# Gates, branch projections, q and k of an encoder block with tokens on partitions, turned back by TensorE

## The chip, the cores and the metric

One core of a Trainium2 chip runs the whole kernel. The metric is the device time in microseconds (us) of one execution, the median of several runs; lower is better. Engines are named as in the profile: PE is TensorE (PEld its weight loads), DVE is VectorE, ACT is ScalarE, POOL is GpSimd and SP is SyncE, which here issues the loads.

## What is computed

One layer of a bidirectional encoder block on 256 tokens of width 2048, all in float32:

```
xn = rms_norm(x, norm_pre_w)
z  = xn @ w_in                      # 2048 x 13312
u_lru, g_lru, q, k, v, g_attn, m_lru, m_attn = split(z)
u   = centred width-4 depthwise conv(u_lru)
h   = rg_lru(u, forward) + rg_lru(u, backward)
y_a = h * silu(g_lru)
q, k = partial_rope(q), partial_rope(k)     # first 32 of 128 dims of each head
y_b = windowed_gqa(q, k, v, sink) * silu(g_attn)    # 16 heads, 4 kv heads, |i-j| <= 128
merged = sigmoid(m_lru) * (y_a @ w_proj_a) + sigmoid(m_attn) * (y_b @ w_proj_b)
out = x + rms_norm(merged @ w_out, norm_post_w)
```

## The kernel before

Every weight is read once, 152 loads of 1 MB each in the order of `load_plan`. Each load is one step, each step two half-steps (hs, 304 in all). To keep float32 accuracy a weight tile is split into a high part wh (a cast on ACT, `parts_of`, L125) and a low part wl (a subtraction on DVE, L126), both in a format that PE multiplies in one pass. Activations are split likewise, and a product is three matmuls: high by high, high by low, low by high. The ring of split weights has five buffers, and the split for half-step hs + 4 is issued in half-step hs; raw loads have three buffers.

There are two ways to make a step:
- A **pair** (`add_pair`) makes 256 output features over two steps. The weights are stationary, the 256 tokens stream, and the result has features on partitions. In the wide form the activation's high and low parts lie side by side, so one 512-column matmul by wh makes two products at once in two halves of a PSUM bank, and a 256-column matmul by wl adds the third (L189, L190, L192); per slice of 128 input features these two alternate. `total` (L201, L202) then adds the two halves. In the narrow form, used for the first four ml pairs and the first gl pair, it is three 256-column matmuls.
- **Rows** (`add_rows`) makes 512 output features over four steps (a "quad" load). A 128-token slice of the activation is stationary, 512 columns of weights stream, and the result has tokens on partitions: 24 matmuls of 512 columns a step (`mm3`, L166 to L168). v and the output projection o are made so.

u's first 512 features have a form of their own (`u_quad`), during which the norm's sum of squares is formed. Until the norm is known, products use xs = x * norm_pre_w, and each pair result is multiplied afterwards by rbc, the reciprocal norm per token (`scaled`, L367); rows use rtok, the same per partition.

The order of all work is written by hand. `at(hs, fn)` and `soon(fn, d)` put work on other engines (and small matmuls on PE) into a half-step, ahead of that half-step's matmuls; each engine then runs its queue strictly in that order. The steps run: u quad; for eight groups ml (four of them), gl, ga, u pairs, with the LRU work of each group (`lru_pair`) spread over about 22 half-steps; k, v; then q pairs with pa and the rest of ml between, beside the 16 heads (`head`), one every four half-steps; then ma and pb, one after the other; then o. Names: ml and ma are the merge gates, gl and ga the silu gates, pa and pb the two branch projections, tm and sm the sigmoids of the merge gates, ms the merged result in two parts.

Of the kernel before, what the change touches and what calls it, by code (L numbers as in the profile page):

```python
# [14 lines left out]
F32 = mybir.dt.float32  # L15
F32R = mybir.dt.float32r
# [11 lines left out]
EPS = 1e-6  # L28
UNITS = 31
EARLY = 4  # L30
AHEAD = 4
DECAY = 12
SPIN = 10
G = 1
LRU0 = 12
HEAD0 = 5
# [15 lines left out]
def load_plan():  # L52

    plan = []

    def quad(m, c):
        plan.extend(("quad", m, c, i) for i in range(4))

    def pair(m, c, n):
        plan.extend(("blk", m, c + (n + i) * P, 0) for i in range(2))  # L60

    quad("w_in", U0)
    for i in range(8):
        if i < EARLY:
            pair("w_in", ML0, 2 * i)
        pair("w_in", GL0, 2 * i)
        pair("w_in", GA0, 2 * i)
        if i < 6:
            pair("w_in", U0, 2 * i + 4)
    pair("w_in", K0, 0)  # L70
    pair("w_in", K0, 2)
    quad("w_in", V0)
    fill = []
    for i in range(8):
        if i >= EARLY:
            fill.append(("w_in", ML0, 2 * i))
        fill.append(("w_proj_a", 0, 2 * i))
    for i in range(4):
        pair("w_in", Q0, 4 * i)
        pair("w_in", Q0, 4 * i + 2)  # L80
        for f in fill[2 * i:2 * i + 2]:
            pair(*f)
    for f in fill[8:]:
        pair(*f)
    for i in range(AHEAD):
        pair("w_in", MA0, 2 * i)
    for i in range(8):
        pair("w_proj_b", 0, 2 * i)
        if i + AHEAD < 8:
            pair("w_in", MA0, 2 * (i + AHEAD))  # L90
    for c in range(4):
        quad("w_out", c * 512)
    return plan


def body(ctx, tc, x, xT, wall, wlru, pvec, npost, ident_d, mask_d, rope_d, out):
# [47 lines left out]
    def soon(fn, d=1):  # L144
        at(now[0] + d, fn)
# [23 lines left out]

    def add_pair(name, act, done, spare=False, wide=True):  # L170


        got = {}

        def half(j, h, wh, wl):
            if j == 0 and h == 0:
                if wide:
                    got["ps"] = banks(name)
                else:
                    got["ps"] = bank(name) if spare else banks(name, (P, 2, S))  # L180
            ps = got["ps"][:, j]
            for k in range(8 * h, 8 * h + 8):
                sl = slice((k % 8) * P, (k % 8 + 1) * P)
                a = act[k // 2][:, k % 2]
                if not wide:
                    mm3(ps, wh[:, sl], wl[:, sl], a[:, 0], a[:, 1], k == 0, k == KT - 1)
                    continue
                if k > 0:
                    nc.tensor.matmul(ps[:, 1], wl[:, sl], a[:, 0], start=False, stop=False)  # L189
                nc.tensor.matmul(ps, wh[:, sl], a, start=k == 0, stop=k == KT - 1)  # L190
                if k == 0:
                    nc.tensor.matmul(ps[:, 1], wl[:, sl], a[:, 0], start=False, stop=False)  # L192
            if j == 1 and h == 1:
                soon(lambda: done(total(got["ps"]) if wide else got["ps"]))

        for j in range(2):
            steps.append(("blk", lambda h, wh, wl, j=j: half(j, h, wh, wl)))

    def total(ps):
        t = half_unit("total", "lo", F32, 1)  # L200
        nc.scalar.copy(t, ps[:, :, 1])  # L201
        nc.vector.tensor_tensor(t, ps[:, :, 0], t, ALU.add)  # L202
        return t

# [53 lines left out]
    mask = const.tile([P, 2, S], F32, name="mask")  # L258
    rope = const.tile([ROT, 2, S], F32, name="rope")
    rbc = const.tile([P, S], F32, name="rbc")  # L260
# [45 lines left out]
    def row_scale():  # L306
# [3 lines left out]
        nc.vector.reciprocal(rbc, rbc)  # L310

    for j in range(4):
        at(j // 2, lambda j=j: scale_x(2, j))
# [16 lines left out]

    at(40, token_scale)

    def load_tables():
        nc.sync.dma_start(ident, ident_d)
        nc.sync.dma_start(mask, mask_d)
        nc.sync.dma_start(rope, rope_d)
# [160 lines left out]
    def silu_evac(units_list, n):  # L497
        def done(ps):
            if n % 4 == 0:
                units_list.append(unit(f"sg{n}"))  # L500
            dst = units_list[n // 4][:, n % 4:n % 4 + 2]
            sg = half_unit(f"sig{n}", "p")
            scaled(dst, ps)
            nc.scalar.activation(sg, dst, AF.Sigmoid)
            nc.vector.tensor_tensor(dst, dst, sg, ALU.mult)
        return done

    tm, sm, ms = [], [], []

    def gate_evac(units_list, n):  # L510
        def done(ps):
            if n % 4 == 0:
                units_list.append(unit(f"mg{n}"))
            t = units_list[n // 4][:, n % 4:n % 4 + 2]
            scaled(t, ps)
            nc.scalar.activation(t, t, AF.Sigmoid)
        return done

    add_ml = lambda i, spare=False: add_pair(f"ml{i}", xs, gate_evac(tm, 2 * i), spare, i >= EARLY)
    b = LRU0  # L520
    for c in range(8):
        if c < EARLY:
            add_ml(c, c == 0)
        add_pair(f"gl{2 * c}", xs, silu_evac(sgl, 2 * c), c == 0, c > 0)
        add_pair(f"ga{2 * c}", xs, silu_evac(sga, 2 * c), c == 0 and EARLY == 0)
        if c < 6:
            n = 2 * c + 4
            add_pair(f"u{n}", xs, lambda ps, n=n: scaled(upad_tile(n)[:, :, 2:2 + S], ps))
        lru_pair(2 * c, b)
        b += 16 if c < EARLY else 12  # L530


    swap = [(i + 16) % 32 for i in range(32)]

    def add_heads(name, then):

        v = {}

        def evac(n):
            def done(ps):  # L540
                v[n] = half_unit(f"{name}f{n}", "uu")
                scaled(v[n], ps)
                for d in range(4):
                    soon(lambda d=d: rotate(n, d), d + 1)
            return done

        def rotate(n, d):
            t = v[n]
            r = t[0:ROT]
            if d == 0:  # L550
                v["s"] = small.tile([ROT, 2, S], F32, tag="upad", name=f"{name}s{n}", bufs=2)
                nc.vector.stream_shuffle(v["s"], r, swap)
                nc.vector.tensor_tensor(r, r, rope[:, 0].unsqueeze(1).to_broadcast([ROT, 2, S]), ALU.mult)
            elif d == 1:
                s = v["s"]
                nc.vector.tensor_tensor(s, s, rope[:, 1].unsqueeze(1).to_broadcast([ROT, 2, S]), ALU.mult)
                nc.vector.tensor_tensor(r, r, s, ALU.add)
            elif d == 2:
                if n == 0:
                    v["h"], v["l"] = unit(f"{name}h", F32R), unit(f"{name}l", F32R)  # L560
                parts_of(v["h"][:, n:n + 2], v["l"][:, n:n + 2], t)
            elif n == 2:
                then(v["h"], v["l"])
                v.clear()

        for n in (0, 2):
            add_pair(f"{name}{n}", xs, evac(n))

    kv = {}
    add_heads("k", lambda h, l: kv.update(kh=h, kl=l))  # L570

# [6 lines left out]

    add_rows("v_ps", xs, v_evac)

# [71 lines left out]

    def add_pa(i):
        def done(ps):
            t = tm[i // 2][:, i % 2 * 2:i % 2 * 2 + 2]
            nc.vector.tensor_tensor(t, ps, t, ALU.mult)

        add_pair(f"pa{i}", ya, done)

    def add_pb(i):  # L660
        def done(ps):
            ms.append(pair_unit(f"ms{i}"))
            t, g = (a[i // 2][:, i % 2 * 2:i % 2 * 2 + 2] for a in (tm, sm))
            nc.vector.tensor_tensor(g, ps, g, ALU.mult)
            nc.vector.tensor_tensor(g, t, g, ALU.add)
            parts_of(ms[i][:, :, 0], ms[i][:, :, 1], g)

        add_pair(f"pb{i}", yb, done)

    add_ma = lambda i: add_pair(f"ma{i}", xs, gate_evac(sm, 2 * i))  # L670
    fill = []
    for i in range(8):
        if i >= EARLY:
            fill.append((add_ml, i))
        fill.append((add_pa, i))
    for i in range(4):
        add_heads(f"q{i}", heads(i))
        for f, n in fill[2 * i:2 * i + 2]:
            f(n)
    for f, n in fill[8:]:  # L680
        f(n)
    for i in range(AHEAD):
        add_ma(i)
    for i in range(8):
        add_pb(i)
        if i + AHEAD < 8:
            add_ma(i + AHEAD)

# [81 lines left out]
def tables():  # L770
# [5 lines left out]
    c, s = np.cos(ang), np.sin(ang)  # L776
    rope = np.stack([np.concatenate([c, c]), np.concatenate([-s, s])], axis=1).astype(np.float32)
    return np.eye(P, dtype=np.float32), np.ascontiguousarray(mask), np.ascontiguousarray(rope)
# [41 lines left out]
```

## Time and profile before

| what | value |
|---|---|
| runs | 922.26 us median of 3 (922.04 to 922.36) |
| profiled execution, first to last instruction (span) | 920.5 us |
| PE busy, share of the span | 910.4 us, 99% |
| DVE busy | 679.9 us, 74% |
| ACT busy | 549.8 us, 60% |
| granted TensorE clock, mean | 0.997 |
| DMA | 172.28 MB, 187 GB/s |

The profile gives the profiled execution's span but no device time of its own; the runs lie 1.5 to 1.9 us above that span. PE's busy time counts overlapping matmuls as one stretch, so it says that PE always had a matmul under way, not how fast they follow each other; that is read from the starts of neighbouring matmuls.

### The profile page before, as it was taken

The page shows a single profiled execution, that of the slowest core. Times are in us where ns is not written, and L with a number is a line of the kernel's source. Part 1 is how long each engine was busy: PE and PEld are TensorE (multiplying, and loading weights), DVE is VectorE, ACT ScalarE, POOL GpSimd, SP SyncE. Part 2 cuts the span into 40 slices and gives each one's busy share as a digit, 9 for nine tenths or more (in the row PEclk, how much of TensorE's full clock was granted, in tenths as well). Part 3 has the DMA queues.
Part 4 walks back from the last instruction along what each step waited for, and adds up shares of the span by engine and source line. Part 5 has one row for each costly group of instructions (what it writes and reads, how often), then busy time and mean ns, then how long its engine had stood idle before and what let it go on. Part 6 is the DMA issues. An engine that isn't in the chain of part 4 may idle for free.

```text
span 920.5 us, 13471 instructions
## 1 busy us (share of the span) xinstructions
PE 910.4 (99%) x5398; PEld 804.2 (87%) x5398; DVE 679.9 (74%) x944; ACT 549.8 (60%) x775; POOL 1.4 (0%) x23
## 2 busy tenths in 40 slices
PE   8999999999999999999999999999999999999996
PEld 8999898988888888888888888888888888888885
DVE  6986868787879888898787868766675566665554
ACT  6758584949597967854544555666554444445451
POOL 0000000000000000000000000000000000000000
PEclk9999999999999999999999999999999999999998
DMA  9755455555464454456544445444555555559542
GB/s 327 256 206 198 141 199 182 207 176 213 142 247 169 165 207 147 162 204 229 183 162 160 143 177 175 146 164 156 183 183 183 185 188 184 192 189 341 185 138 91
DMA packets 27614, 172.28 MB, mean 187 GB/s; under 512 B 3072, under 2 KB 3840, under 8 KB 8480
## 3 DMA queue, kind: packets, MB, share of 16 engines
q1 hardware_dynamic: 26832, 170.27, 52.3%
q10 hardware_dynamic: 720, 1.16, 0.3%
q8 instruction: 42, 0.69, 0.3%
q14 instruction: 20, 0.16, 0.0%
HBM read 169.32 MB, written 2.10 MB: 186 GB/s over the span
## 4 chain that ended last, share of the span: by engine, by line
PE 98%; DMA 1%; DVE 0%; ACT 0%; SPq 0%; DVEq 0%; issue 0%
PE pb L190 7%; PE ga L190 7%; PE ma L190 6%; PE q L190 6%; PE pa L190 6%; PE gl L190 6%; PE u L190 5%; PE o L168 4%; PE o L167 4%; PE o L166 4%; PE ml L190 3%; PE pb L189 3%; PE ga L189 3%; PE ma L189 3%; PE pa L189 3%; PE q L189 3%
## 5 line engine op out<-in xcount | busy, mean ns | idle before, releaser
L126 DVE TENSOR_TENSOR wl<-raw,wh 128x1024 fp32r<-128x1024 f32 (+1 forms) x306 | 368.8, 1214 | 166.2 <-ACT wh L125 165.5
L125 ACT CAST wh<-raw 128x1024 fp32r<-128x1024 f32 (+1 forms) x305 | 312.5, 1042 | 118.8 <-PE o L168 31.1
L190 PE MATMUL ga<-xs,wh 128*128 128x512 f32 x256 | 90.5, 397 | 0.0
L190 PE MATMUL pb<-yb,wh 128*128 128x512 f32 x256 | 90.0, 398 | 0.0
L190 PE MATMUL ma<-xs,wh 128*128 128x512 f32 x256 | 89.9, 397 | 0.0
L190 PE MATMUL pa<-ya,wh 128*128 128x512 f32 x256 | 89.9, 396 | 0.0
L190 PE MATMUL q<-xs,wh 128*128 128x512 f32 x256 | 89.7, 396 | 0.0
L190 PE MATMUL gl<-xs,wh 128*128 128x512 f32 x224 | 78.9, 397 | 0.0
L189 PE MATMUL pb<-yb,wl 128*128 128x256 f32 x240 | 67.5, 281 | 0.0
L189 PE MATMUL ma<-xs,wl 128*128 128x256 f32 x240 | 67.4, 281 | 0.0
L189 PE MATMUL ga<-xs,wl 128*128 128x256 f32 x240 | 67.4, 281 | 0.0
L190 PE MATMUL u<-xs,wh 128*128 128x512 f32 x192 | 67.2, 395 | 0.0
L189 PE MATMUL q<-xs,wl 128*128 128x256 f32 x240 | 67.1, 279 | 0.0
L189 PE MATMUL pa<-ya,wl 128*128 128x256 f32 x240 | 67.1, 279 | 0.0
L189 PE MATMUL gl<-xs,wl 128*128 128x256 f32 x210 | 58.9, 280 | 0.0
L190 PEld LDWEIGHTS pb<-yb,wh 128*128 128x128 f32 x256 | 47.4, 188 | 10.5
L190 PEld LDWEIGHTS ga<-xs,wh 128*128 128x128 f32 x256 | 47.6, 188 | 10.2
L190 PEld LDWEIGHTS ma<-xs,wh 128*128 128x128 f32 x256 | 47.4, 188 | 10.2
L190 PEld LDWEIGHTS q<-xs,wh 128*128 128x128 f32 x256 | 47.4, 188 | 9.8
L190 PEld LDWEIGHTS pa<-ya,wh 128*128 128x128 f32 x256 | 47.4, 188 | 9.7
L189 PE MATMUL u<-xs,wl 128*128 128x256 f32 x180 | 50.3, 279 | 0.0
L166 PE MATMUL o<-wh,ms 128*128 128x512 f32 x128 | 49.8, 389 | 0.0
(267 smaller groups left out, 1958.0 us busy)
## 6 DMA issues: line engine op xcount, KB each, us to landing
raw<-wall_dram SPq DMA_DIRECT2D x149, 1024.0 KB, 4.8
lraw<-wlru_dram SPq DMA_DIRECT2D x8, 512.0 KB, 5.7
raw<-wall_dram SPq DMA_DIRECT2D x4, 512.0 KB, 7.6
xr<-x_dram SPq DMA_DIRECT2D x4, 512.0 KB, 10.2
raw<-wall_dram SPq DMA_DIRECT2D x4, 256.0 KB, 4.8
xT<-xT_dram SPq DMA_DIRECT2D x4, 256.0 KB, 7.0
np<-npost_dram SPq DMA_DIRECT2D x2, 512.0 KB, 8.0
out_dram<-yw SPq DMA_DIRECT2D x4, 256.0 KB, 2.3
```

The source lines that it names most:

```text
L125: cast(h, src)
L126: nc.vector.tensor_tensor(l, src, h.bitcast(F32), ALU.subtract)
L166: nc.tensor.matmul(ps, wh, xh, start=start, stop=False)
L167: nc.tensor.matmul(ps, wh, xl, start=False, stop=False)
L168: nc.tensor.matmul(ps, wl, xh, start=False, stop=stop)
L189: nc.tensor.matmul(ps[:, 1], wl[:, sl], a[:, 0], start=False, stop=False)
L190: nc.tensor.matmul(ps, wh[:, sl], a, start=k == 0, stop=k == KT - 1)
```

## The change

ml, ma, pa, pb, k and q become rows: 84 of the 152 steps go from the pair form to the rows form. gl, ga and the later u groups stay pairs. Where the features are needed on partitions afterwards (q and k for the scores, the merged result for o), PE turns the result with 128x128 transposes against the identity. x is normalised once: after the norm is known xT is scaled by norm_pre_w and rbc and split into xn, which later steps use instead of xs; the scaling of each pair result falls away. The rotary embedding works on token rows (`rotate`). In pairs the wide matmuls of a half-step come in a run of eight and the narrow ones in another, arranged so that runs of neighbouring half-steps join. The order of steps changes: u quad, ml's first quad, v, then the groups with the other ml quads between, k, then q and pa in turn, ma, pb, o.

```diff
-UNITS = 31
-EARLY = 4
-AHEAD = 4
+UNITS = 32
-LRU0 = 12
+LRU0 = 13
+BETWEEN = {1: 1, 3: 2, 5: 3}
+XN = 15
+PACE = (20,) + (16,) * 6 + (12,) * 2
...
     quad("w_in", U0)
+    quad("w_in", ML0)
+    quad("w_in", V0)
...
+    quad("w_in", K0)
+    for c in range(4):
+        quad("w_in", Q0 + c * 512)
+        quad("w_proj_a", c * 512)
+    for c in range(4):
+        quad("w_in", MA0 + c * 512)
+    for c in range(4):
+        quad("w_proj_b", c * 512)
...
-    def add_pair(name, act, done, spare=False, wide=True):
+    def add_pair(name, act, done):
...
+            def row(wide):
+                for k in range(8 * h, 8 * h + 8):
+                    sl = slice((k % 8) * P, (k % 8 + 1) * P)
+                    a = act[k // 2][:, k % 2]
+                    if wide:
+                        nc.tensor.matmul(ps, wh[:, sl], a, start=k == 0, stop=k == KT - 1)
+                    else:
+                        nc.tensor.matmul(ps[:, 1], wl[:, sl], a[:, 0], start=False, stop=False)
+
+            row(h == 0)
+            row(h == 1)
...
+    def weigh(i):
+        for j in range(4):
+            nc.scalar.activation(xt[i][:, j], xt[i][:, j], AF.Copy, scale=norm(4 * i + j))
+
+    def normal(i):
+        t = xt[i]
+        nc.vector.tensor_tensor(t, t, rbc.unsqueeze(1).to_broadcast([P, 4, S]), ALU.mult)
+
+    def xn_parts(i):
+        for j in range(2):
+            a = pair_unit(f"xn{2 * i + j}")
+            xn.append(a)
+            parts_of(a[:, :, 0], a[:, :, 1], xt[i][:, 2 * j:2 * j + 2])
+
+    for i in range(4):
+        at(7 + 2 * i, lambda i=i: weigh(i))
+        at(XN + 2 * i, lambda i=i: normal(i))
+        at(XN + 1 + 2 * i, lambda i=i: xn_parts(i))
...
-    at(40, token_scale)
+    at(ROWS + 3, token_scale)
+    at(6, lambda: nc.sync.dma_start(ident, ident_d))
...
+        def evac(t, ps):
+            if t == 0:
+                v["t"] = unit(f"{name}t", F32, (P, 2, 512))
+            nc.scalar.copy(v["t"][:, t], ps)
+            if t == 1:
+                soon(rotate)
+                soon(flip, 2)
+                for q in range(2):
+                    soon(lambda q=q: part(q), 3 + q)
...
+            nc.vector.tensor_tensor(m[:, :, :, 0:half], r[:, :, :, half:ROT], table(1, 0, half), ALU.mult)
+            nc.vector.tensor_tensor(m[:, :, :, half:ROT], r[:, :, :, 0:half], table(1, half, ROT), ALU.mult)
+            nc.vector.tensor_tensor(c, r[:, :, :, 0:ROT], table(0, 0, ROT), ALU.mult)
+            nc.vector.tensor_tensor(r[:, :, :, 0:ROT], c, m, ALU.add)
...
+        def flip():
+            for q in range(2):
+                v[q] = bank(f"{name}p{q}")
+                for j in range(2):
+                    n = 2 * q + j
+                    for t in range(2):
+                        nc.tensor.transpose(v[q][:, j, t * P:(t + 1) * P], v["t"][:, t, n * P:(n + 1) * P], ident)
...
+    def add_pb(c):
+        held = {}
+        def done(t, ps):
+            g = sm[c][:, t]
             nc.vector.tensor_tensor(g, ps, g, ALU.mult)
+            nc.vector.tensor_tensor(g, tm[c][:, t], g, ALU.add)
+            if t == 1:
+                soon(flip)
+                for q in range(2):
+                    soon(lambda q=q: part(q), 2 + q)
```

The order on PE in the pairs that stay. In the rows below a name is out<-streamed,stationary; gl is the PSUM tile, xs and xn the activation, wh and wl the weight parts. Before, the start of a gl pair:

```order
L190 MATMUL gl_1105<-xs_120,wh_0_975 128x512
L192 MATMUL gl_1105<-xs_120,wl_0_976 128x256
L189 MATMUL gl_1105<-xs_120,wl_0_976 128x256
L190 MATMUL gl_1105<-xs_120,wh_0_975 128x512
L189 MATMUL gl_1105<-xs_131,wl_0_976 128x256
L190 MATMUL gl_1105<-xs_131,wh_0_975 128x512
```

And now:

```order
L175 MATMUL gl_881<-xn_639,wh_0_761 128x512 x2
L175 MATMUL gl_881<-xn_642,wh_0_761 128x512 x2
L175 MATMUL gl_881<-xn_692,wh_0_761 128x512 x2
L175 MATMUL gl_881<-xn_695,wh_0_761 128x512 x2
L177 MATMUL gl_881<-xn_639,wl_0_762 128x256 x2
L177 MATMUL gl_881<-xn_642,wl_0_762 128x256 x2
```

Wide and narrow matmuls no longer alternate; sixteen of one kind follow sixteen of the other.

On DVE in the pb stage, where the merged result is formed and split (total is the sum of the two PSUM halves, mg a gate tile, ms the parts). Before:

```order
L202 TENSOR_TENSOR total<-pb_6904,total 128x512
L664 TENSOR_TENSOR mg_6601<-total,mg_6601 128x512
L665 TENSOR_TENSOR mg_6601<-mg_580,mg_6601 128x512
L126 TENSOR_TENSOR ms_6988<-mg_6601,ms_6988 128x2x256
L126 TENSOR_TENSOR wl_0_6994<-raw_6941,wh_0_6993 128x1024
```

And now, for one quad of pb; PE's two rows of four transposes each (`ms_ps<-ident,mg`, L694) stand a half-step behind the last L682 and ahead of that half-step's matmuls:

```order
L116 TENSOR_TENSOR wl_1_6601<-raw_6548,wh_1_6600 128x1024
L681 TENSOR_TENSOR mg_5936<-pb__6485,mg_5936 128x512
L682 TENSOR_TENSOR mg_5936<-mg_651,mg_5936 128x512
L681 TENSOR_TENSOR mg_5936<-pb__6485,mg_5936 128x512
L682 TENSOR_TENSOR mg_5936<-mg_651,mg_5936 128x512
L116 TENSOR_TENSOR wl_0_6623<-raw_6582,wh_0_6622 128x1024
L116 TENSOR_TENSOR wl_1_6650<-raw_6582,wh_1_6649 128x1024
L116 TENSOR_TENSOR ms_6667<-ms_ps_6639,ms_6667 128x2x256
```

PE now waits for DVE's four products before it turns the tile, and the split of ms moves behind the turn.

On DVE near half-steps 14 to 16, while the first LRU group starts (uu is the convolution, sp the decay constants, lwl the LRU weights' low part). Before:

```order
L424 SCALAR_TENSOR_TENSOR uu_575<-upad_535,pv,uu_575 128x256 x3
L126 TENSOR_TENSOR wl_1_619<-raw_501,wh_1_618 128x1024
L387 TENSOR_TENSOR sp_e<-sp_e,sp_den 128x32
L388 TENSOR_TENSOR sp_s_166<-sp_e 128x32
L126 TENSOR_TENSOR lwl_651<-lraw_442,lwh_650 128x1024
L126 TENSOR_TENSOR wl_0_655<-raw_571,wh_0_654 128x1024
L389 TENSOR_SCALAR sp_pl<-sp_s_166 128x32
```

And now:

```order
L432 SCALAR_TENSOR_TENSOR uu_569<-upad_513,pv,uu_569 128x256 x3
L116 TENSOR_TENSOR wl_0_599<-raw_537,wh_0_598 128x1024
L307 TENSOR_TENSOR xT_96<-xT_96,rbc 128x1024
L397 TENSOR_SCALAR sp_pl<-sp_s_166 128x32
L389 SCALAR_TENSOR_TENSOR sp_pl<-sp_pl,sp_s_166 128x32
L116 TENSOR_TENSOR lwl_618<-lraw_469,lwh_617 128x1024
L116 TENSOR_TENSOR wl_1_622<-raw_537,wh_1_621 128x1024
L116 TENSOR_TENSOR xn_639<-xT_96,xn_639 128x2x256
L116 TENSOR_TENSOR xn_642<-xT_96,xn_642 128x2x256
```

The multiplication by rbc and two subtractions for xn now stand between the weight splits, and the same again three more times.

More of the change, by code (lines that the diff above doesn't have):

```diff
@@ L62, in load_plan @@
     quad("w_in", U0)
+    quad("w_in", ML0)
+    quad("w_in", V0)
     for i in range(8):
-        if i < EARLY:
-            pair("w_in", ML0, 2 * i)
         pair("w_in", GL0, 2 * i)
@@ L69, in load_plan @@
             pair("w_in", U0, 2 * i + 4)
[L70 to L90, printed above, removed]
+        if i in BETWEEN:
+            quad("w_in", ML0 + BETWEEN[i] * 512)
+    quad("w_in", K0)
[6 more added lines that the diff above has]
+        quad("w_proj_b", c * 512)
     for c in range(4):
@@ L176, in half, with total @@
             if j == 0 and h == 0:
[L177 to L180, printed above, removed]
+                got["ps"] = banks(name)
             ps = got["ps"][:, j]
[L182 to L192, printed above, removed]
+            def row(wide):
[8 more added lines that the diff above has]
+            row(h == 1)
             if j == 1 and h == 1:
-                soon(lambda: done(total(got["ps"]) if wide else got["ps"]))
+                soon(lambda: done(got["ps"]))
         for j in range(2):
             steps.append(("blk", lambda h, wh, wl, j=j: half(j, h, wh, wl)))
-    def total(ps):
+    def total(dst, ps):
         t = half_unit("total", "lo", F32, 1)
         nc.scalar.copy(t, ps[:, :, 1])
-        nc.vector.tensor_tensor(t, ps[:, :, 0], t, ALU.add)
-        return t
+        nc.vector.tensor_tensor(dst, ps[:, :, 0], t, ALU.add)
     def add_rows(name, act, done, spare=False, last=False):
@@ L258, in body @@
     mask = const.tile([P, 2, S], F32, name="mask")
-    rope = const.tile([ROT, 2, S], F32, name="rope")
+    rope = const.tile([P, 2, 2, ROT], F32, name="rope")
     rbc = const.tile([P, S], F32, name="rbc")
@@ L310, in row_scale @@
         nc.vector.reciprocal(rbc, rbc)
+    xn = []
+    def weigh(i):
[13 more added lines that the diff above has]
+        at(XN + 1 + 2 * i, lambda i=i: xn_parts(i))
     for j in range(4):
@@ L329, in token_scale @@
             nc.scalar.activation(dg, dg, AF.Copy, accum_out=rtok[:, t:t + 1])
-    at(40, token_scale)
+    at(ROWS + 3, token_scale)
+    at(6, lambda: nc.sync.dma_start(ident, ident_d))
     def load_tables():
-        nc.sync.dma_start(ident, ident_d)
         nc.sync.dma_start(mask, mask_d)
@@ L502, in done, with u_evac @@
             sg = half_unit(f"sig{n}", "p")
-            scaled(dst, ps)
+            total(dst, ps)
             nc.scalar.activation(sg, dst, AF.Sigmoid)
-            nc.vector.tensor_tensor(dst, dst, sg, ALU.mult)
+            soon(lambda: nc.vector.tensor_tensor(dst, dst, sg, ALU.mult))
         return done
+    def u_evac(n):
+        return lambda ps: total(upad_tile(n)[:, :, 2:2 + S], ps)
     tm, sm, ms = [], [], []
[L510 to L516, printed above, removed]
-        return done
@@ L519, in body @@
[L519 to L530, printed above, removed]
@@ L533, in body @@
[L533 to L567, printed above, removed]
@@ L569, in body, with gate_evac @@
+    def gate_evac(units_list, c, scale=1.0):
+        def done(t, ps):
+            if t == 0:
+                units_list.append(unit(f"mg{c}", F32, (P, 2, 512)))
+            nc.scalar.activation(units_list[c][:, t], ps, AF.Sigmoid, scale=rtok[:, t:t + 1] if scale is None else scale)
+        return done
+    add_rows("ml0_", xs, gate_evac(tm, 0, None), True)
     kv = {}
-    add_heads("k", lambda h, l: kv.update(kh=h, kl=l))
     def v_evac(t, ps):
@@ L577, in v_evac @@
         nc.vector.scalar_tensor_tensor(vl, ps, rtok[:, t:t + 1], vh.bitcast(F32), ALU.mult, ALU.subtract)
-    add_rows("v_ps", xs, v_evac)
+    add_rows("v_", xs, v_evac)
+    b = LRU0
+    for c in range(8):
+        add_pair(f"gl{2 * c}", xn, silu_evac(sgl, 2 * c))
+        add_pair(f"ga{2 * c}", xn, silu_evac(sga, 2 * c))
+        if c < 6:
+            add_pair(f"u{2 * c + 4}", xn, u_evac(2 * c + 4))
+        if c in BETWEEN:
+            add_rows(f"ml{BETWEEN[c]}_", xn, gate_evac(tm, BETWEEN[c]))
+        lru_pair(2 * c, b)
+        b += PACE[c]
@@ new lines, in add_heads, with rotate, part @@
+    def add_heads(name, then):
+        v = {}
+        def evac(t, ps):
+            if t == 0:
+                v["t"] = unit(f"{name}t", F32, (P, 2, 512))
[5 more added lines that the diff above has]
+                    soon(lambda q=q: part(q), 3 + q)
+        def rotate():
+            r = v["t"].rearrange("p t (h d) -> p t h d", h=4)
+            both = small.tile([P, 2, 2, 4, ROT], F32, tag="turn", name=f"{name}r", bufs=1)
+            c, m = both[:, 0], both[:, 1]
+            table = lambda i, a, b: rope[:, :, i, a:b].unsqueeze(2).to_broadcast([P, 2, 4, b - a])
+            half = ROT // 2
+            nc.vector.tensor_tensor(m[:, :, :, 0:half], r[:, :, :, half:ROT], table(1, 0, half), ALU.mult)
[9 more added lines that the diff above has]
+                        nc.tensor.transpose(v[q][:, j, t * P:(t + 1) * P], v["t"][:, t, n * P:(n + 1) * P], ident)
+        def part(q):
+            if q == 0:
+                v["h"], v["l"] = unit(f"{name}h", F32R), unit(f"{name}l", F32R)
+            parts_of(v["h"][:, 2 * q:2 * q + 2], v["l"][:, 2 * q:2 * q + 2], v[q])
+            if q == 1:
+                then(v["h"], v["l"])
+                v.clear()
+        add_rows(f"{name}_", xn, evac)
@@ L581, in head @@
+    add_heads("k", lambda h, l: kv.update(kh=h, kl=l))
     def head(hd, qh, ql, b):
@@ L650, in heads, with add_pa, done, flip @@
         return then
[L653 to L675, printed above, removed]
+    def add_pa(c):
+        def done(t, ps):
+            g = tm[c][:, t]
+            nc.vector.tensor_tensor(g, ps, g, ALU.mult)
+        add_rows(f"pa{c}_", ya, done)
+    def add_pb(c):
+        held = {}
+        def done(t, ps):
+            g = sm[c][:, t]
+            nc.vector.tensor_tensor(g, ps, g, ALU.mult)
+            nc.vector.tensor_tensor(g, tm[c][:, t], g, ALU.add)
[3 more added lines that the diff above has]
+                    soon(lambda q=q: part(q), 2 + q)
+        def flip():
+            for q in range(2):
+                held[q] = bank(f"ms_ps{c}{q}")
+                for j in range(2):
+                    n = 2 * q + j
+                    for t in range(2):
+                        nc.tensor.transpose(held[q][:, j, t * P:(t + 1) * P], sm[c][:, t, n * P:(n + 1) * P], ident)
+        def part(q):
+            a = pair_unit(f"ms{2 * c + q}")
+            ms.append(a)
+            parts_of(a[:, :, 0], a[:, :, 1], held.pop(q))
+        add_rows(f"pb{c}_", yb, done)
     for i in range(4):
         add_heads(f"q{i}", heads(i))
[L678 to L684, printed above, removed]
+        add_pa(i)
+    for i in range(4):
+        add_rows(f"ma{i}_", xn, gate_evac(sm, i))
+    for i in range(4):
         add_pb(i)
-        if i + AHEAD < 8:
-            add_ma(i + AHEAD)
     npt, xr, yw = [], [[], []], [[], []]
@@ L776, in tables @@
     c, s = np.cos(ang), np.sin(ang)
-    rope = np.stack([np.concatenate([c, c]), np.concatenate([-s, s])], axis=1).astype(np.float32)
+    rope = np.stack([np.concatenate([c, c]), np.concatenate([-s, s])]).astype(np.float32)
+    rope = rope.reshape(2, ROT, 2, P).transpose(3, 2, 0, 1)
     return np.eye(P, dtype=np.float32), np.ascontiguousarray(mask), np.ascontiguousarray(rope)
```

## The prediction

> **What bounds the kernel now.** I read the page's first block and chain, then PE's own waits, then the chain in order of time, because what matters is how long PE needs from one product to the next.
>
> ```profile
> PE 910.4 (99%) x5398; PEld 804.2 (87%) x5398; DVE 679.9 (74%) x944; ACT 549.8 (60%) x775; POOL 1.4 (0%) x23
> PE 98%; DMA 1%; DVE 0%; ACT 0%; SPq 0%; DVEq 0%; issue 0%
> PE u_ps L352 <- ACT wh L125: 1.5, 2, 0.9
> ACT wh L125 <- PE pb L190: 14.2, 8, 1.8
> 912.86 0.24 PE o L168
> ```
>
> PE is the chain: 98% of the span, and its longest wait (two times, 1.5 us in all) lies in the first steps. ACT waits for PE to hand back weight buffers, so the weight path runs ahead of PE. From PE's last product (913.10) to the end at 920.5 lie 7.4 us that the change doesn't touch. So the question is PE's time per step, plus any new wait. A step is one MB of weights. It has two forms: 16 slices of a 512-column and a 256-column matmul (pair), or 24 matmuls of 512 columns (rows); both stream 12,288 columns.
>
> ```profile
> 684.65 0.46 PE ma L190 x2
> ...
> 692.40 0.24 PE pb L190
> 692.64 0.12 PE pb L189
> 692.76 0.23 PE pb L190
> ...
> 707.24 0.46 PE ma L190 x2
> L166 PE MATMUL o<-wh,ms x128: 389/389/389, 825.9 to 912.2; 128*128 128x512 f32 x128
> ```
>
> The first and last rows are the same place of two pairs, four steps apart: 22.59 us, so a wide pair step takes 5.648 us, 353 ns a slice. The o row gives the other form: one of three matmuls, 127 intervals in 86.3 us, 679.5 ns for three, 226.5 ns each; a rows step takes 5.44 us. PE is "busy" in both, so busy time doesn't show the difference.
>
> ```profile
> 42.80 0.28 PE L166 MATMUL gl<-xs,wh 128*128 128x256 f32 x1
> ...
> 50.72 0.28 PE L166 MATMUL gl<-xs,wh 128*128 128x256 f32 x1
> 368.49 0.28 PE L166 MATMUL gate<-uh,lwh 128*128 128x256 f32 x1
> ...
> 369.79 0.28 PE L168 MATMUL gate<-uh,lwl 128*128 128x256 f32 x1
> 370.07 0.24 PE v_ps L166
> 372.14 0.23 PE v_ps L166
> ```
>
> Runs of narrow matmuls: 66 intervals in 7.92 us (120 ns) and 11 in 1.30 us (118 ns). A narrow pair step (48 of them; the first four ml pairs and gl0) takes 5.76 us. The two v_ps rows are nine matmuls apart: 230 ns each for wide ones just after narrow ones, before they settle at 226.5.
>
> **Part 1: ml, ma, pa, pb, k and q as rows (84 of 152 steps).** ma and pb: 32 steps, 5.648 - 5.44 = 0.208 each, 6.6 us. k: 4 steps, 0.8. The narrow ml pairs: 8 steps, 0.32 each, 2.6. q, pa and the last ml pairs lie among the heads:
>
> ```profile
> 451.63 0.60 PE L616 MATMUL pt<-ident,p 128*128 128x128 f32 x4
> 451.99 0.36 PE L166 MATMUL sc<-kh,q0h 128*128 128x256 f32 x1
> 452.79 0.28 PE L189 MATMUL q<-xs,wl 128*128 128x256 f32 x1
> 451.80 0.44 PE pt L616 x4
> ...
> 647.30 0.44 PE pt L616 x4
> 450.00:655.00 205.00, 205.00 (x1258) 182.01 (x1257) 156.81 (x298) 114.18 (x188) 0.00 (x0) 1.00 0.47 165
> ```
>
> Fifteen heads in 195.5 us are 13.03 us each; of that 1.16 is pt and sc (451.63 to 452.79) and six o matmuls take 0.71, which leaves 5.58 for a step. So 40 steps gain 0.14: 5.6. Part 1 gives 15.6 us.
>
> **Part 2: pairs that stay (gl, ga, u), with wide and narrow matmuls in runs.** 44 steps. No row shows such a run of 16 and 16; bounds come from the rows above: 16 x (226.5 + 118) = 5.51 us and 16 x (230 + 120) = 5.60. I take 228.5 and 119, 5.56: a run begins as v_ps does and then settles. 42 wide steps gain 0.088 and gl0's two 0.2: 4.1 us (2.5 to 6.2; nothing, if the mix isn't what costs).
>
> **Part 3: the turns on PE.** Nine flips (k, four q, four pb) of eight 128x128 transposes: 72, all on the path. pt is the same instruction. The chain gives 0.44 us for four, 110 ns; from the starts (451.63 to 451.99) it is 90. I take 110: 7.9 us (6.5 to 8.3). The Trainium skill (TensorE: Matmul & The Clock Gate, Part 4: PE-mode transpose) puts one at about 275 ns in a kernel and says the full clock doesn't engage for it. The trace agrees with the length alone: 0.60 us from the first start to the last end of four which start 0.36 apart with their follower, and in the window 450 to 655, with 15 heads' transposes, the granted clock is 1.00. By the page's figure the flips would be an estimated 19.8 us.
>
> **Part 4: what DVE, ACT and the queues get.**
>
> ```profile
> L126 DVE TENSOR_TENSOR wl<-raw,wh 128x1024 fp32r<-128x1024 f32 x302 | 366.0, 1221 | 164.9 <-ACT wh L125 164.2
> L125 ACT CAST wh<-raw 128x1024 fp32r<-128x1024 f32 x302 | 310.6, 1047 | 117.6 <-PE o L168 31.1 <-PE ma L190 18.5 <-PE pb L190 14.2
> L367 DVE TENSOR_TENSOR sg<-total,rbc 128x512 f32<-128x512 f32 x15 | 10.4, 693 | 0.5
> L491 DVE TENSOR_TENSOR gi<-gi,th 128x1024 f32<-128x1024 f32 x8 | 9.7, 1218 | 0.0
> L126 DVE TENSOR_TENSOR yb<-sg,yb 128x512 fp32r<-128x512 f32 x8 | 5.5, 684 | 0.0
> L280 ACT ACTIVATE xs<-xT,pv 128x256 fp32r<-128x256 f32 x16 | 7.4, 503 | 3.5 <-DMA xT<-xT_dram 1.8 <-DMA pv<-pvec_dram 1.5
> L424 DVE SCALAR_TENSOR_TENSOR uu<-upad,pv,uu 128x256 f32<-128x256 f32 x48 | 23.3, 485 | 2.6 <-DVE uu L424 0.5
> ACT L309 <- PE rps L308: 2.4, 1, 2.4
> 27.43 1.22 DVE L299 TENSOR_TENSOR sq<-sq,sq 128x1024 f32<-128x1024 f32 x1
> 28.56 1.22 DVE L126 TENSOR_TENSOR wl<-raw,wh 128x1024 fp32r<-128x1024 f32 x1
> 48.54 1.23 DVE L126 TENSOR_TENSOR wl<-raw,wh 128x1024 fp32r<-128x1024 f32 x1 [1.63 <-ACT wh L125]
> ```
>
> Added once: xn, on ACT 16 scalings (503 ns) and 8 casts (somewhat over half of L125's 1.05, about 0.6), 13 us; on DVE 4 multiplies (nearest 1218) and 8 subtractions (684), 10.4 us. Removed: the L367 scaling of 48 pairs, 33 us of DVE, and the totals of what becomes rows; nothing of that was on the path. The new work is bunched in half-steps 7 to 22, and in 13 to 24 it meets the first LRU pair. There I count on DVE 12 splits, 4 multiplies, 8 subtractions, the convolution (8 of about 0.47, 3.7), lwl, ul, v, gated and small ones: some 37 us of durations, less 0.09 of overlap for each of 45 (27.43 to 28.56 is 1.13 for 1.22), so 33. PE needs 12 x 2.72 and 24 gate matmuls, 35.4. ACT comes to about the same 33, its table loads counted. That is 93%, with ACT and DVE waiting for each other. What covers it is the lead: the split at 48.54 is for half-step 16 and ends at 49.8; half-step 12 began at 42.80, and four narrow ones of 2.88 later is 54.3, a lead of 4.5. Served in turn, the lead shrinks to about 1 us near half-steps 20 and 28. I charge 0.5 (0 to 6).
>
> The scaling stands ahead of L309's Sqrt on ACT, which idled 2.4 us there for PE; it fits. ident's load moves from half-step 20 to 6 on SP's queue, ahead of one raw load; 64 KB among 1 MB loads that come two steps early: nothing. rope keeps its place and bytes.
>
> Each flip makes PE wait for other engines, with a whole half-step queued behind. For k and q the order is copy (half-step +1), rope (+2), flip (+3): DVE has PE's whole half-step for four small products (about 1.5 us). For pb it is tight:
>
> ```profile
> 690.00:825.00 135.00, 135.00 (x767) 117.26 (x766) 83.51 (x87) 62.53 (x72) 0.00 (x0) 1.00 0.53 185
> 748.38 0.69 DVE L664 TENSOR_TENSOR mg<-total,mg 128x512 f32<-128x512 f32 x1
> 749.10 0.69 DVE L665 TENSOR_TENSOR mg<-mg,mg 128x512 f32<-128x512 f32 x1
> ```
>
> Four products (two dependent pairs at 0.72 and 0.69, about 2.8 us) against PE's 2.72. But token half 0 is complete six matmuls (1.36 us) earlier, so DVE can begin before the half-step ends. I charge 0.1 for each of four, 0.4. For the last pb, o needs it four half-steps later.
>
> **Sum.** 15.6 + 4.1 - 7.9 - 0.5 - 0.4 = 10.9 us. The profiled span of 920.5 becomes 909.6. The runs (median 922.26) lie 1.8 us above the span, for what is outside it: **911.4 us**. As a check, adding steps for the kernel before in the same way comes to about 1 us more than its span.
>
> **Rivals.**
> - The jam: DVE and ACT lose the lead at half-steps 13 to 32 and PE waits 3 to 6 us. For: 93% load in turns. Against: durations overlap, and pairs after it need less DVE than before. 914 to 917.
> - Grouping gains nothing: the extra of the mix comes from narrow matmuls however they stand. For: they take 118 to 120 in runs, no less than beside wide ones. Against: the wide ones take 226.5 in runs and about 234 in the mix (353 less 119). 915.5.
> - Slower: the flips expose the whole chain ahead of them, because DVE comes to it only when its split is done. Each wait is then up to 2.8 us, nine of them 25 us: 935. It decides from 1.2 us a flip. Against: DVE is busy 84 of 135 us in the pb stage.
> - The change doesn't do what it says: time goes by columns alone, rows gain nothing, and the flips are added: about 931. The rows of 353 and 226.5 ns speak against it. The Trainium skill's rule (same page, Back-to-back issue gap: N/2.4 + 2.5 ns) gives just this, an estimated 5.20 us against 5.18 a step; the trace doesn't agree.
> - Transposes one after another at their whole length of 272 ns (0.60 less 0.33): 19.6 us, 923. pt's starts speak against it; the page on transposes stands nearest to it.
>
> **Chances.** Forecast (908 to 913.5) 0.62, jam 0.15, no gain by grouping 0.1, lower by cheap turns and runs 0.05; slower flips 0.03, columns alone 0.02, long transposes 0.03. A measurement here tells 0.2%, 1.8 us, from no change. Faster 0.92, same 0.02, slower 0.06. Range: low, 1.8 more from Part 2, 1.4 from cheaper turns, no waits: 907; high, the jam at 6: 917. Outside are some 0.15.
>
> **What would show it.** Rows cadence of 227 ns in pa and pb; a pair step of gl at 5.5 to 5.6; eight transposes in about 0.9 us; no wait of PE before L694's and L583's transposes over 0.3 us; DVE nearly full from 45 to 85 us without a PE wait. I am wrong if PE waits for wl or wh there, or if the pair steps stay at 5.65.

## The result, and the profile after

| kernel | time, median (range) | ratio to before, 95% interval | span |
|---|---|---|---|
| before | 922.15 us (921.61 to 922.36) | 1 | 920.5 us |
| changed | 914.65 us (914.31 to 915.47) | 0.9921 [0.9906, 0.9935] | 912.5 us |

The change gains 7.5 us, and 8.0 us of the profiled span; forecast were 10.9 us, and 911.4 us with a range of 907 to 917. The measured time lies in that range, but above the 908 to 913.5 that was given a chance of 0.62. The first rows of the changed kernel's page: busy time by engine, then the chain by engine.

```profile
PE 903.0 (99%) x4638; PEld 772.1 (85%) x4638; DVE 610.6 (67%) x841; ACT 551.7 (60%) x775; POOL 1.4 (0%) x23
PE 98%; DMA 1%; DVE 0%; ACT 0%; issue 0%; SPq 0%; DVEq 0%
```

PE is still the chain; that DVE has 69 us less to do lies off it. PE's waits in the changed kernel (total us, times, longest):

```profile
PE spin L240 <- POOL eps L235: 1.0, 1, 1.0
PE u_ps L360 <- ACT wh L115: 0.8, 2, 0.5
PE kp L583 <- issue: 0.4, 1, 0.4
```

Only kp is new: the turn of k, whose wait is over the 0.3 us that the prediction had named as its limit. Next, PE's timeline (start, us, name, xcount) for a pair that stays, and the rows by tile (min/median/max ns of one, first and last start):

```profile
384.43 2.08 PE L177 MATMUL gl<-xn,wl 128*128 128x256 f32 x16
386.34 3.82 PE L175 MATMUL gl<-xn,wh 128*128 128x512 f32 x16
389.99 2.08 PE L177 MATMUL gl<-xn,wl 128*128 128x256 f32 x16
```

```profile
L156 PE MATMUL pb__6485<-wh,yb x32: 389/389/389, 726.5 to 747.6; 128*128 128x512 f32 x32
L158 PE MATMUL ml__1518<-wh,xn x32: 389/389/389, 147.6 to 168.6; 128*128 128x512 f32 x32
L156 PE MATMUL ml__2370<-wh,xn x32: 389/389/389, 241.4 to 262.5; 128*128 128x512 f32 x32
```

From narrow run to narrow run a pair step takes 389.99 - 384.43 = 5.56 us, the value taken. pb has one L156 in three matmuls: 31 intervals in 21.1 us, 227 ns a matmul, 5.45 us a step. Between the two ml quads, from 168.6 to 241.4, lie 12 pair steps and the gate matmuls of two LRU groups: 72.8 us, a yardstick for the experiments.

The turns, from the chain in order of time of the changed kernel (start, us, what):

```profile
435.15 0.44 issue
435.58 1.06 PE kp L583 x8
458.45 0.88 PE q0p L583 x8
490.00 0.44 PE pt L632 x4
502.80 0.44 PE pt L632 x4
751.13 0.11 PE ms_ps L694
751.24 0.98 PE ms_ps L694 x7
774.13 0.98 PE ms_ps L694 x7
```

A turn of eight takes 0.87 to 0.88 us where nothing is waited for. kp takes 0.44 + 1.06, and each pb turn 0.11 + 0.98: 1.09. The second transpose of a turn reads the other token half, and that is where pb's 0.2 us lies; the view of waits doesn't list it.

DVE in half-steps 13 to 24 (stretch; us; PE, PEld, DVE, ACT, POOL busy and count; clock, DMA share, GB/s):

```profile
45.00:55.00 10.00, 10.00 (x45) 8.28 (x45) 9.18 (x18) 6.02 (x12) 0.14 (x2) 1.00 0.54 202
55.00:65.00 10.00, 10.00 (x51) 8.49 (x50) 9.38 (x17) 8.34 (x12) 0.00 (x0) 1.00 0.30 107
65.00:75.00 10.00, 10.00 (x52) 8.49 (x52) 9.90 (x18) 7.01 (x13) 0.00 (x0) 1.00 0.68 243
```

DVE is 92 to 99% busy, and PE is busy throughout.

### The profile page after: what moved, and what is told of

It reads as the page before. It is cut to its first block, busy times and chain, and to the rows that moved or that the text cites. A ratio compares the mean times of both kernels' runs of the same rounds, so it can differ in the third digit from the quotient of the medians.

```text
span 912.5 us, 11845 instructions
## 1 busy us (share of the span) xinstructions
PE 903.0 (99%) x4638; PEld 772.1 (85%) x4638; DVE 610.6 (67%) x841; ACT 551.7 (60%) x775; POOL 1.4 (0%) x23
## 4 chain that ended last, share of the span: by engine, by line
PE 98%; DMA 1%; DVE 0%; ACT 0%; issue 0%; SPq 0%; DVEq 0%
PE ga L175 6%; PE gl L175 6%; PE u L175 5%; PE o L156 4%; PE o L158 4%; PE o L157 4%; PE ga L177 3%; PE gl L177 3%; PE u L177 3%; PE u_ps L360 2%; PE gate L156 1%; PE gate L158 1%; PE gate L157 1%; PE ma__6163 L156 1%; PE pa__5483 L156 1%; PE ma__5943 L156 1%
## 5 line engine op out<-in xcount | busy, mean ns | idle before, releaser
L175 PE MATMUL gl<-xn,wh 128*128 128x512 f32 x256 | 62.5, 391 | 0.0
L175 PE MATMUL ga<-xn,wh 128*128 128x512 f32 x256 | 62.5, 391 | 0.0
L175 PEld LDWEIGHTS gl<-xn,wh 128*128 128x128 f32 x256 | 46.8, 188 | 9.0
L175 PEld LDWEIGHTS ga<-xn,wh 128*128 128x128 f32 x256 | 46.8, 188 | 9.0
L156 PE MATMUL o<-wh,ms 128*128 128x512 f32 x128 | 49.9, 390 | 0.0
L158 PE MATMUL o<-wh,ms 128*128 128x512 f32 x128 | 49.8, 389 | 0.0
L157 PE MATMUL o<-wl,ms 128*128 128x512 f32 x128 | 49.8, 389 | 0.0
L175 PE MATMUL u<-xn,wh 128*128 128x512 f32 x192 | 46.8, 391 | 0.0
L175 PEld LDWEIGHTS u<-xn,wh 128*128 128x128 f32 x192 | 35.3, 188 | 6.8
L177 PE MATMUL ga<-xn,wl 128*128 128x256 f32 x256 | 33.7, 283 | 0.0
L158 PEld LDWEIGHTS o<-wh,ms 128*128 128x128 f32 x128 | 24.0, 188 | 5.0
L156 PEld LDWEIGHTS o<-wh,ms 128*128 128x128 f32 x128 | 24.0, 188 | 4.9
```

The lines of the kernel that those rows point to most:

```text
L156: nc.tensor.matmul(ps, wh, xh, start=start, stop=False)
L157: nc.tensor.matmul(ps, wh, xl, start=False, stop=False)
L158: nc.tensor.matmul(ps, wl, xh, start=False, stop=stop)
```

## The experiments

Each was timed beside runs of the kernel before on the same chip; diffs are against the changed kernel unless said otherwise.

**The pairs alternate again (e1).** It undoes Part 2 alone.

```diff
-            row(h == 0)
-            row(h == 1)
+            for k in range(8 * h, 8 * h + 8):
+                ...
+                if k > 0:
+                    nc.tensor.matmul(ps[:, 1], wl[:, sl], a[:, 0], start=False, stop=False)
+                nc.tensor.matmul(ps, wh[:, sl], a, start=k == 0, stop=k == KT - 1)
+                if k == 0:
+                    nc.tensor.matmul(ps[:, 1], wl[:, sl], a[:, 0], start=False, stop=False)
```

> The changed kernel with the wide and narrow matmuls of the gl, ga and u pairs alternating again as before (44 steps). Theory A (runs are cheaper): each of the 44 steps goes from 5.56 us back to 5.61 to 5.65, so 2.2 to 4.0 us slower than the changed kernel, 917 to 918.6 us. Rival (the order inside a pair doesn't matter, all gain is from rows): 914.6 us within 0.9.

Measured: 916.27 us, 0.9936 [0.9924, 0.9949], span 914.7. Its rows of the two ml quads:

```profile
L158 PE MATMUL ml__1518<-wh,xn x32: 388/389/390, 148.4 to 169.5; 128*128 128x512 f32 x32
L156 PE MATMUL ml__2370<-wh,xn x32: 388/389/390, 242.8 to 263.9; 128*128 128x512 f32 x32
```

169.5 to 242.8 is 73.3 us, 0.5 more than with runs over the same 12 steps. Runs are worth 0.04 us a step here, 1.6 us by the medians and 2.2 us of span in all. The time lies between the two that were expected (917 to 918.6, and at most 915.5): the order matters, but by less than 2.2 us in the runs. The cause is in the trace of before (PE timeline, the first low-part matmul of four steps; then two windows, with the granted clock third from the end):

```profile
68.67 0.27 PE L192 MATMUL u<-xs,wl 128*128 128x256 f32 x1
74.22 0.28 PE L192 MATMUL u<-xs,wl 128*128 128x256 f32 x1
96.92 0.28 PE L192 MATMUL gl<-xs,wl 128*128 128x256 f32 x1
102.57 0.28 PE L192 MATMUL ga<-xs,wl 128*128 128x256 f32 x1
68.00:79.00 11.00, 11.00 (x67) 9.71 (x67) 6.89 (x10) 9.69 (x17) 0.00 (x0) 1.00 0.57 220
91.00:102.00 11.00, 11.00 (x65) 9.57 (x65) 9.12 (x15) 6.20 (x7) 0.14 (x2) 1.00 0.34 108
```

The first two are one step apart, 5.55 us; the next two also, 5.65. The same code runs at two cadences, 347 and 353 ns a slice. Of the 42 wide steps among gl, ga and u 14 are fast: in seven places the pair that begins right behind gate matmuls. The other 28 are slow, also those behind narrow ml matmuls. e1 repeats this, with 12 fast steps of 44. The prediction had sized all of them from the ma and pb stage, which runs at 353 from 667.8 us on.

**Runs in the kernel before (e2).** It does Part 2 alone; against the kernel before.

```diff
-            for k in range(8 * h, 8 * h + 8):
-                ...
+            for high in ((h == 0, h == 1) if wide else (None,)):
+                for k in range(8 * h, 8 * h + 8):
+                    ...
+                    elif high:
+                        nc.tensor.matmul(ps, wh[:, sl], a, start=k == 0, stop=k == KT - 1)
+                    else:
+                        nc.tensor.matmul(ps[:, 1], wl[:, sl], a[:, 0], start=False, stop=False)
```

> The kernel before with one edit: in its wide pairs (118 steps) the matmuls of a half-step stand in a run of eight wide and a run of eight narrow. Theory A: 0.05 to 0.09 us a step, 6 to 10 us, so 912 to 916 us; that would be as fast as the whole change, and rows with their turns would be worth nothing beyond it. Rival (rows are what pays, the runs pay at most 4 us): 918 to 922 us.

Measured: 917.55 us, 0.9951 [0.9937, 0.9964], 4.6 us by the medians and between the two times expected. The span of 914.7 is 5.8 us shorter, but about 1 us of that is an earlier start (see e8): 4.8 us for 118 wide steps, 0.04 each. PE in the pb stage of that kernel:

```profile
688.30 2.08 PE L191 MATMUL pb<-yb,wl 128*128 128x256 f32 x16
690.21 3.82 PE L189 MATMUL pb<-yb,wh 128*128 128x512 f32 x16
693.86 2.08 PE L191 MATMUL pb<-yb,wl 128*128 128x256 f32 x16
```

5.56 us again. So a few lines in the old kernel bring 4.6 of the 7.5 us; rows, turns and xn together add 2.9 beyond that.

**Every turn made twice (e3).**

```diff
-                    for t in range(2):
+                    for t in (0, 1, 0, 1):
```

> The changed kernel with each of the 72 transposes of the flips issued twice into the same place. Theory A (110 ns each, all on PE's path): 7.9 us slower, about 922.5 us; with 90 ns each 921. Rival (each at its whole length of 272 ns): 19.6 us slower, 934. Rival (most of a flip's price is the wait for DVE before it): under 5 us slower, below 919.6.

Measured: 922.2 us, 1.0002 [0.9993, 1.0011], span 920.1: 7.6 us for 72 transposes, 106 ns each. From its chain, and the lengths of single ones (min/median/max ns):

```profile
508.18 1.75 PE q1p L583 x16
755.23 1.97 PE ms_ps L694 x16
L694 PE MATMUL ms_ps<-ident,mg x64: 272/273/328, 755.1 to 828.2; 128*128 128x128 f32 x64
```

Sixteen take 1.75, twice 0.87. The Trainium skill (TensorE: Matmul & The Clock Gate, Part 4: PE-mode transpose) gives about 275 ns for one in a kernel; the run agrees with that for the length of one and not for the price of one in a row.

**xs in place of xn (e4).** The products take x without its norm, so that ACT and DVE have nothing to do for xn.

```diff
-    xn = []
+    xn = xs
...
-    for i in range(4):
-        at(7 + 2 * i, lambda i=i: weigh(i))
-        at(XN + 2 * i, lambda i=i: normal(i))
-        at(XN + 1 + 2 * i, lambda i=i: xn_parts(i))
```

> The changed kernel without the scaling, normalising and splitting that make xn: the products read xs, so the results lack the norm. Theory A (that work is hidden by the lead of the weight splits): 914.6 us within 0.9, PE without a wait either way. Rival (the jam at half-steps 13 to 32 costs PE time): 1 to 4 us faster, 911 to 913.5.

Measured: 914.25 us, 0.9914 [0.9901, 0.9928], span 912.4. One of its windows, and its one wait beyond the start:

```profile
65.00:75.00 10.00, 10.00 (x51) 8.46 (x50) 4.19 (x6) 6.62 (x15) 0.00 (x0) 1.00 0.53 205
```

```profile
PE kp L579 <- issue: 0.4, 1, 0.4
```

DVE falls from 9.90 to 4.19 us of ten, and the span by 0.1. The jam cost nothing that shows.

**k and q as pairs in runs (e5).** ml, ma, pa and pb stay rows; the old rope on features comes back.

```diff
-    quad("w_in", K0)
+    pair("w_in", K0, 0)
+    pair("w_in", K0, 2)
...
-        quad("w_in", Q0 + c * 512)
+        pair("w_in", Q0, 4 * c)
+        pair("w_in", Q0, 4 * c + 2)
...
-        add_rows(f"{name}_", xn, evac)
+        for n in (0, 2):
+            add_pair(f"{name}{n}", xn, evac(n))
```

> The changed kernel with k and q made as pairs in runs (features on partitions, rope as before, no flip); ml, ma, pa, pb stay rows. Theory A (a turn of 512 features costs 0.88 us on PE and rows save 4 x 0.11 us against pairs in runs): k and q save five flips of 0.88 and k's extra wait of 0.6, 5.0 us, and give back 20 x 0.11, 2.2 us: 2.8 us faster than the changed kernel, 911.9 us. Rival (rows are worth 0.2 a step, as against the alternating pairs): 914.6 us within 1.

Measured: 911.77 us, 0.9888 [0.9872, 0.9903], span 909.8, as expected. Rows are 0.11 us a step shorter than pairs in runs (5.56 less 5.45), 2.2 us over these 20 steps, and their five turns take 4.4 us and kp's wait 0.6.

**Later turns (e6, e7).** e6 is e5 with pb's turn one half-step later; e7 is the changed kernel with that and k's turn one later too. The lines of both in pb (e7 in the same way for k):

```diff
-                soon(flip)
+                soon(flip, 2)
                 for q in range(2):
-                    soon(lambda q=q: part(q), 2 + q)
+                    soon(lambda q=q: part(q), 3 + q)
```

> As e5_qk_pairs, and pb's flips (with the splits behind them) one half-step later, so that DVE has finished when PE comes to them. Theory A (0.2 us of each pb flip is a wait for DVE's four products): 0.8 us faster than e5_qk_pairs, 911.1 us. Rival (the 0.2 is what PE pays around any turn): the same as e5_qk_pairs within 0.5.

> The changed kernel with k's flip and pb's flips one half-step later. Theory A: k's 0.6 and pb's 4 x 0.2 us go, 1.4 us, 913.2 us; eight transposes then take 0.88 us everywhere. Rival (no wait, only the turns' own price): 914.6 us.

Measured: e6 910.51 us, 0.9873 [0.9859, 0.9886], span 908.8; e7 912.57 us, 0.9896 [0.9883, 0.991], span 910.7. The turns of e7 in its chain:

```profile
437.62 0.88 PE kp L584 x8
752.95 0.87 PE ms_ps L695 x8
```

Every turn is at 0.87 to 0.88. 1.8 us of span are gone, 1.6 of them behind the start (see e8), near the 1.5 that the waits come to. e6 is the fastest kernel of this study, 4.1 us under the changed one.

**The changed kernel again (e8)**, unedited.

> The changed kernel itself, beside the others on the same chip: 914.65 us within 0.6.

Measured: 914.91 us (914.01 to 915.69), 0.9922 [0.9909, 0.9934], span 913.0. The spans of its five runs go from 912.2 to 913.9, which bounds what small differences of medians and spans can say. Between the profiles the difference lies at the start, before the first matmul of ml (PE timeline of the changed kernel, of e8 and of e4):

```profile
30.51 0.40 PE L156 MATMUL ml<-wh,xs 128*128 128x512 f32 x1
30.97 0.40 PE L156 MATMUL ml<-wh,xs 128*128 128x512 f32 x1
30.36 0.40 PE L156 MATMUL ml<-wh,xs 128*128 128x512 f32 x1
```

From there to the end all three take 882.0 us. The kernel before, with that matmul at 30.86, takes 889.6. Counted like this the change gains 7.6 us and e2 4.8 (from 29.94), e1 loses 2.1 (from 30.58), and e4 differs from the changed kernel by less than 0.1.

**Runs of two, and wide first (e9, e10, e11, e12).** What makes an alternating stream slow in some stages? e9 makes runs of two (wide, wide, narrow, narrow); e10 alternates with the wide matmul always first; e11 does e10's edit in the kernel before, e12 in e6.

```diff
+            for k in range(8 * h, 8 * h + 8):
+                ...
+                nc.tensor.matmul(ps, wh[:, sl], a, start=k == 0, stop=False)
+                nc.tensor.matmul(ps[:, 1], wl[:, sl], a[:, 0], start=False, stop=k == KT - 1)
```

> The changed kernel with the pairs' matmuls in runs of two (two wide, two narrow) instead of eight. If each step from narrow to wide costs a little, a pair step lies between the two forms, 5.60 us, and the kernel at 915.5 us; if the slow cadence is a state that only strict alternation falls into, the step stays at 5.55 to 5.56 and the kernel at 914.7.

> The changed kernel with the pairs' matmuls alternating, wide ahead of narrow in every slice (the kernel before has it so in the first slice only), so that wl is first needed one wide matmul later and a step ends on a narrow one. If alternation itself is what can run at 353 ns a slice, this gives steps of 5.65 among steps of 5.55, as e1_alternate, 916.3 us; if the order at a step's ends sets the slow cadence, steps of 5.55 only and 914.6 us.

> The kernel before with one edit in its wide pairs (118 steps): wide ahead of narrow in every slice, so that no two wide and no two narrow matmuls meet at a step's ends. If the slow cadence comes from those ends, all steps run at about 346 to 347 ns a slice, 5.54 us, 0.07 a step less: 8 us faster than before, 914 us, as fast as the whole change. If e10_wide_first only had it by the rows beside its pairs, 917 to 922 us.

> e6_qk_pairs_late (k and q as pairs, pb's flips a half-step later) with the pairs alternating, wide first (64 steps), instead of in runs. At 346 ns a slice against 348, 0.02 a step: 1.3 us faster, 909.2 us. If runs and wide-first alternation are worth the same, 910.5 us.

Measured: e9 914.44 us, 0.9913 [0.9895, 0.993]; e10 914.92, 0.9919 [0.9901, 0.9936]; e11 920.14, 0.9977 [0.9969, 0.9986]; e12 911.43, 0.9881 [0.9865, 0.9897]. Runs of two do as well as runs of sixteen, and in the changed kernel wide first alternates as fast as runs go. In the kernel before it gains 2.0 us, not the 4.6 of the runs. Two places of e11, each from one wide matmul to the ninth after it:

```profile
404.81 0.40 PE L188 MATMUL q<-xs,wh 128*128 128x512 f32 x1
...
407.99 0.40 PE L188 MATMUL q<-xs,wh 128*128 128x512 f32 x1
739.75 0.39 PE L188 MATMUL pb<-yb,wh 128*128 128x512 f32 x1
...
742.86 0.40 PE L188 MATMUL pb<-yb,wh 128*128 128x512 f32 x1
```

Each is nine slices: 3.18 us (353 ns) in q, 3.11 (346 ns) in pb. The order at a step's ends, which e10 seemed to blame, doesn't decide it, since e11 has it and runs at both. What does stays open. e12 (span 910.0) took longer than either time expected and doesn't beat e6.

## Why the prediction was right, and where it was off

The mechanism of the likeliest case came about: faster, by the rows, less the turns. Its size did not: 914.65 us lies above that case's 908 to 913.5 and within the jam's 914 to 917, though there was no jam (e4). The terms, in us of span:

| term | forecast | found |
|---|---|---|
| Part 1, rows | +15.6 | +14.6 |
| Part 2, runs | +4.1 | +2.2 (e1: 2.1) |
| Part 3, turns | -7.9 | -7.9 (nine of 0.875; e3: 7.6) |
| jam | -0.5 | 0 (e4: 0.1) |
| waits for DVE | -0.4 | -1.5 (e7: 1.6) |
| start, 0.4 earlier by chance (e8) | 0 | +0.4 |
| sum | +10.9 | +7.8, measured 8.0 |

**Part 1** held. The one part under it is q, pa and the last ml, 40 steps among the heads: from pt to pt (490.00 to 502.80) a head takes 12.80 us, where it took 13.03, so a step gains 0.115 and not 0.14. By such steps the term is 14.3. The 14.6 adds up, from each matmul's start to the next one's, the matmuls of ml, k, q, pa, ma and pb: 473.2 us before and 459.8 after, in which 0.4 is the wait for k's turn and 0.8 are the ends of the turns.

**Part 2 is the step that failed in size.** The new price, 5.56, held. The 2.2 is the same sum over gl, ga and u, 247.4 us before and 245.2 after. The old price was not: I took 5.648 from the ma and pb stage for pairs that lie among gl, ga and u, where a third of the steps ran at 5.55. By e1 and e2 the gain is 0.04 to 0.05 us a step in place of 0.088. The rows of before at 68.67 and 74.22, quoted under e1, would have shown it.

**The waits failed too, by a wrong assumption.** I let DVE begin on token half 0 before the half-step ends. DVE's timeline of the changed kernel, at the first pb (in brackets the idle time before, and whom it waited for):

```profile
748.44 0.69 DVE L681 TENSOR_TENSOR mg<-pb__6485,mg 128x512 f32<-128x512 f32 x1 [0.41 <-PE pb__6485 L158]
749.16 0.69 DVE L682 TENSOR_TENSOR mg<-mg,mg 128x512 f32<-128x512 f32 x1
749.77 0.68 DVE L681 TENSOR_TENSOR mg<-pb__6485,mg 128x512 f32<-128x512 f32 x1
750.49 0.69 DVE L682 TENSOR_TENSOR mg<-mg,mg 128x512 f32<-128x512 f32 x1
```

DVE stood idle for 0.41 us until pb's last matmul and then needed 748.44 to 751.18, 2.74 us, against PE's 2.72 of a half-step. Both token halves lie in one PSUM tile. In o each half has a tile of its own, and there ACT in the same trace reads each half as it is done, the second 1.36 us, six matmuls, after the first:

```profile
838.65 0.60 ACT L733 ACTIVATE junk<-o 128x512 f32<-128x512 f32 x1 [0.30 <-PE o L158]
840.01 0.60 ACT L733 ACTIVATE junk<-o 128x512 f32<-128x512 f32 x1 [0.67 <-PE o L158]
```

So the shared tile fits as the reason why DVE waits for the last matmul; pb with separate tiles was not run. k had been forecast to have slack, and had none:

```profile
427.65 1.28 ACT L498 ACT_TABLE_LOAD   x1
433.06 1.23 DVE L116 TENSOR_TENSOR wl<-raw,wh 128x1024 fp32r<-128x1024 f32 x1 [0.69 <-ACT wh L115]
434.20 0.28 DVE L572 TENSOR_TENSOR kr<-kt,rope 128x128 f32<-128x128 f32 x1
435.06 0.42 DVE L575 TENSOR_TENSOR kt<-kr 128x256 f32<-128x256 f32 x1
```

The last LRU group's table load and Sqrt stand ahead of the weight casts on ACT there. DVE's split at 433.06 waited 0.69 us for such a cast, and the rope behind it ends at 435.48, when PE has stood for the turn since 435.15. That the table load is what made the casts late is read from the order alone. The rival of exposed turns was thus true in kind, at 0.2 to 0.6 us for five of nine turns, far from the 1.2 at which it decides.

**Part 3** and the rivals: columns alone and long transposes are excluded by 227 ns a matmul and e3's 106 ns. "Grouping gains nothing" is excluded by e1 and e2, though half true: an alternating stream can run as fast as runs do. **The jam** was overcharged: DVE was 99% busy and PE did not wait, so the lead, which the prediction had put at 4.5 us, was enough.

Of the miss of 3.2 us the span makes up 2.9. The rest comes from the choice of the execution: the profiled one, 914.31 us, was the fastest of four and 0.34 below their median. What lies outside its span is 1.8 us, as taken.

## What to carry to other kernels

Before pricing a stream of equal instructions, read its cadence in every stage that the change touches: one stage's 5.65 us a step stood for steps of which a third took 5.55. A layout that spares 0.11 us a step must be set against its turn of 0.88 us for 512 features. Over four steps it is a loss, as e5 shows for q and k, and even the slower pace, 0.2 us a step, would not quite pay for it. It is a gain where several products share one turn: ml, pa, ma and pb together have 16 steps for each turn, 1.8 us against 0.88 by these prices. Before placing a transpose behind another engine's work, count that engine's whole chain after the last matmul, and its queue ahead of it; one half-step more was free here (e6, e7).

## What the runs showed of the hardware

- An alternating stream of 512- and 256-column matmuls ran at 346 to 347 or at 353 ns a pair in the same program (before and e11) and kept a pace for half a step or for many; runs of two, eight or sixteen gave 348. Neither the order at a step's ends (e11) nor the granted clock, 1.00 in the windows of both paces under e1, explains it.
- Back to back, 128x128 transposes cost 106 to 110 ns each though one lasts 272; in the window of 450 to 655 us of the kernel before, with the transposes of 15 heads, the granted clock is 1.00.
- DVE at 92 to 99% and ACT at 60 to 83% busy for 30 us did not make PE wait once.
